# Two more sets of seven block products, third blocks asked for earlier, and more partner half tiles

## The chip, the cores and the metric

The kernel runs on one core of one Trainium2 chip. The metric is the device time of one execution in microseconds (us), as a median of runs. Five engines work on a core, each in its own program order, and wait for one another through semaphores: TensorE (PE in the profile, with its weight loads as PEld), VectorE (DVE), ScalarE (ACT), GpSimd (POOL) and SyncE (SP). DMA transfers are issued here by SP, by POOL and a few by ACT; a DMA stands in its issuer's queue, and a wait of the DMA holds what stands behind it in that queue.

## What is computed

One decoder layer on 256 tokens of width 2048, in float32 (cut to what matters):

```
h    = rmsnorm(x, pre_norm_g)                       # 256 x 2048
proj = h @ w_in                                     # a_q a_k a_v a_g a_lr b_q b_k b_v b_g m_a m_b
gk   = log_sigmoid(a_lr @ gla_gk_w2 + gla_gk_b) / 16
o_a  = rmsnorm(gated_linear_attention(a_q, a_k, a_v, gk), gla_norm_g) * silu(a_g)
o_b  = rmsnorm(differential_attention(b_q, b_k, b_v, lam), diff_norm_g) * (1 - lam_init) * silu(b_g)
merged = sigmoid(m_a) * (o_a @ w_branch_a) + sigmoid(m_b) * (o_b @ w_branch_b)
x + rmsnorm(merged @ w_out, post_norm_g)
```

The projection has 18,448 columns, the three matrices behind it 2048 each. The differential attention has 16 heads; the kernel treats them in four groups g of four, and each group in two pairs.

## The kernel before, in words

**Split operands.** A float32 product is made of three TensorE products: weights and activations are each split into a rounded part (hi) and the rest (lo), and hi*hi, hi*lo and lo*hi are added in PSUM. The x side is split once (tiles `xs`). Each weight is split as it comes: half a tile of 128x2048 at a time, ACT writes `hi` (L236) and DVE subtracts to get `lo` (L237). Both have three buffers, and the splits of a half tile are written four half tiles ahead of its matmuls (`AHEAD`, `take`).

**Plain half tiles.** `token_major` (matmuls on L413) makes 512 columns for the 256 tokens: eight half tiles of 12 matmuls. `channel_major` (L433 and L435) makes 128 columns with tokens along the free axis: two half tiles of 16 matmuls each.

**Block products.** A *set* makes two 256x512 results from one 2048x1024 weight with the 2x2 scheme that needs seven block products in place of eight (`PRODUCTS`, order 1, 3, 5, 6, 2, 7, 4). Each product has four half tiles of six matmuls (L666). The weight is cut into four blocks: `a` and `b` are tiles of 128x2048 by SP (`link`, four buffers), `c` is loaded by SP in four pieces of 128x1024 (L181) when product 2 reaches the split, and another block is added into `a` after product 1 and into `b` after product 6 by a DMA that accumulates, issued by POOL (L193). DVE makes a+b for product 6 (L184) and adds c into a behind each split of product 2 (L191). Product 4 accumulates into the same PSUM bank that DVE has just read for product 7.

**The joint phase.** Three sets run (`SETS = 3`): two for the branch-b merge gate, one for the values and gates (`dv0`, `bg0`) of head group 0. `phase_steps` puts *partner* half tiles between their 84 steps, spread evenly: `v4` (8 half tiles, token major) and `k` and `q` of the linear attention (32, channel major), 40 in all. Results of the sets go to DRAM by `spill` (a DMA on POOL) and come back by `fetch` (POOL too).

**After the phase.** Four `ag` tiles, m00, m01, head groups 0 and 1, the branch-a product `y0`, head groups 2 and 3, m02, m03, then `y1` and `o`. Groups 1 to 3 make `dv` and `bg` as plain tiles. Between half tiles `pump` lets small tasks go one step on: the forget gate, the scores and outputs of the linear attention, the attention pairs (`diff_pair`: scores L877/878, maxima on DVE L882, exponentials on ACT L888, weights L895, transposes L899, values L907 to L909, norm with a power on POOL L327, L920, transposes L925). In front of half tile 6 of the first `y1` tile, `settle` runs all tasks that are left to their end. A scheduling layer then settles the order on each engine.

Of the kernel before, what the change touches and what calls it, by code (L numbers as in the profile page):

```python
# [14 lines left out]
P = 128  # L15
# [13 lines left out]
SETS = 3  # L29
# [57 lines left out]
def hybrid_kernel(ctx: ExitStack, tc, xt, xn, preg, postg, w, w2, gkb, glag, lamv, diffg, ident_d, causal_d, lmask_d, out):  # L87
# [60 lines left out]
    def heads_order(g):  # L148
        values = (f"dv{g}", f"bg{g}") if g + 2 >= SETS else ()
        return halves_of(*values, *(f"{name}{g}{c}" for pair in range(2) for name in ("dq", "dk") for c in (2 * pair, 2 * pair + 1)))  # L150
# [20 lines left out]
    def emit_set(s, prod, t, h):  # L171
# [7 lines left out]
        if prod == 2:  # L179
            raws[s, t, h] = u([P, 1024], "c")  # L180
            sp.dma_start(raws[s, t, h], weights(f"set{s}", 4 + t)[0][:, c])  # L181
# [417 lines left out]
    ts = {}  # L599

    def others():
# [7 lines left out]
        for hf in range(2):  # L609
            for name in ("k", "q"):  # L610
                ts[name, hf] = u([P, 2, 4, P], name)
                for c in range(4):
                    o = ps("bg")
                    for h in range(2):
                        half_channel(o, h, *take(f"{name}{hf}{c}"))
                        if h:
                            o1, o2 = (t.rearrange("p (b t) -> p b t", b=2) for t in (o[:, :S], o[:, S:]))
                            t = ts[name, hf][:, :, c, :]
                            act.activation(t, o2, AF.Copy)
                            dve.tensor_tensor(out=t, in0=o1, in1=t, op=ALU.add)  # L620
# [10 lines left out]
    def block_products(s):  # L631
        x = ps("mm")
        bank = {1: x, 6: x, 7: x, 4: x}
        left, right = u([P, 2, 512], "gl"), u([P, 2, 512], "gr")
        kept = {}

        def right_done(b):
            dst = right[:, b, :]
# [7 lines left out]
        def left_done(b, src):  # L646
            if s < 2:
                act.activation(left[:, b, :], src, AF.Tanh, scale=half_rstd[:, b : b + 1])
            else:
                act.activation(left[:, b, :], src, AF.Copy, scale=rstd[:, b : b + 1])  # L650

        for prod in PRODUCTS:
# [3 lines left out]
            for t in range(2):  # L656
                for h in range(2):
# [10 lines left out]
                    if t and h:  # L668
# [6 lines left out]
                        if prod == 6:  # L675
                            dve.tensor_tensor(out=right[:, 0, :], in0=x, in1=kept[3], op=ALU.add)
                            right_done(0)
                        if prod == 2:
                            dve.tensor_tensor(out=left[:, 0, :], in0=out, in1=kept[1], op=ALU.add)
                            left_done(0, left[:, 0, :])  # L680
                        if prod == 7:
                            dve.tensor_tensor(out=right[:, 1, :], in0=x, in1=kept[5], op=ALU.add)
                            right_done(1)
                            gspill[2 * s + 1] = spill(right, "gr")
                        if prod == 4:
                            left_done(1, x)
                            gspill[2 * s] = spill(left, "gl")
# [20 lines left out]
    def gla_scores(hf, q, k):  # L708
# [80 lines left out]
    for hf in range(2):  # L789
        tasks.append(gla_scores(hf, ts["q", hf], ts["k", hf]))  # L790
# [58 lines left out]
    def diff_split(g, pair, tq, tk, q2, kh, kl):  # L849
# [11 lines left out]
    def diff_pair(g, pair, q2, kh, kl, vv, uu):  # L861
        oh, ol = obh[g], obl[g]
        cm = causal.rearrange("p a t -> p (a t)")
        cuts = ((0, P), (P, 3 * P))
        while f"split{g}{pair}" not in done:
            yield
        for h in (2 * pair, 2 * pair + 1):
# [60 lines left out]
        split_out(bank, hi, lo, diffg_s)  # L928
        yield

    def diff_heads(g):
        if g + 2 < SETS:
            vv, uu = (fetch(gspill[2 * g + 4 + i], name, u) for i, name in enumerate(("dv", "ub")))
        else:
# [7 lines left out]
            for b in range(2):  # L942
                gate(banks[b], b, uu[:, b, :])
        obh.append(u2([P, 4, S], "obh", F32R))
        obl.append(u2([P, 4, S], "obl", F32R))
        for pair in range(2):
            ts = []
            for name in ("dq", "dk"):
                t = t2([P, 2, S], name)
                for c in range(2):  # L950
                    o, o2 = channel_major(f"{name}{g}{2 * pair + c}")
                    act.activation(t[:, c, :], o2, AF.Copy)
# [214 lines left out]
```

## Time and profile before

| | |
|---|---|
| median of 3 runs | 1133.51 us (1131.94 to 1133.74) |
| the profiled execution | 1133.58 us, span 1131.8 us |
| busy | PE 1117.8, DVE 784.2, ACT 653.6, POOL 77.5 us |
| matmuls | 5618 |
| DMA | 234.68 MB, mean 207 GB/s |
| joint phase in the trace | about 82 to 309 us |

The span is the time between the first and the last recorded instruction; 1.8 us of the execution lie outside. Busy TensorE time counts a matmul from its start to a modelled end, so consecutive matmuls overlap in it: the step from one matmul of 512 columns to the next is shorter than the mean duration shown for one. The granted clock (PEclk) is 1.00 at full speed. A line `A <- B` in a list of waits reads: A stood idle until B was done. In a timeline the note in brackets is the idle time before the instruction and what ended it.

### The profile page before, as it was taken

To read this page: it belongs to the slowest core of one execution; us is meant where nothing else is said; L and a number is where in the kernel's file an instruction comes from. 1 tells how busy PE (TensorE), PEld (TensorE's weight loads), DVE (VectorE), ACT (ScalarE), POOL (GpSimd) and SP (SyncE) were. 2 spreads that over 40 slices of the span, in tenths; PEclk is the share of its full clock that TensorE was granted. 3 is DMA by queue.
4 is the path that set the end of the run, shared out by engine and by line. 5 is a ranking of instruction groups with operands and counts; after the bars stand their busy time and mean duration, and the time that the engine had idled before them with its cause. 6 is when DMAs were issued, how large, how long until landed. Compare 5 with 4: busy or idle time off the path is not lost.

```text
span 1131.8 us, 14913 instructions
## 1 busy us (share of the span) xinstructions
PE 1117.8 (99%) x5618; PEld 957.4 (85%) x5618; DVE 784.2 (69%) x1112; ACT 653.6 (58%) x971; POOL 77.5 (7%) x109
## 2 busy tenths in 40 slices
PE   9999999999999999999999999999999999999996
PEld 8998888887888888888888888888888888888886
DVE  6878979778757996856676555557666765666463
ACT  7856766665666564656676455556655655444460
POOL 0101010001102100101010100000000100000000
PEclk9999999999999999999999999999999999999999
DMA  8799897687454556764455545555455565556752
GB/s 302 256 409 240 264 291 212 246 257 195 156 197 168 198 177 223 236 243 151 160 193 176 211 161 183 183 186 186 155 180 186 195 214 183 180 188 212 276 188 75
DMA packets 39512, 234.68 MB, mean 207 GB/s; under 512 B 4944, under 2 KB 6480, under 8 KB 16912
## 3 DMA queue, kind: packets, MB, share of 16 engines
q1 hardware_dynamic: 31968, 202.79, 50.6%
q0 software_dynamic: 6464, 29.63, 9.8%
q10 hardware_dynamic: 1008, 1.32, 0.4%
q8 instruction: 44, 0.72, 0.3%
q14 instruction: 28, 0.23, 0.1%
HBM read 223.23 MB, written 10.49 MB: 207 GB/s over the span
## 4 chain that ended last, share of the span: by engine, by line
PE 94%; DVE 2%; DMA 1%; issue 1%; ACT 1%; SPq 0%; DVEq 0%; POOLq 0%; POOL 0%; ACTq 0%
PE mm L413 51%; PE mm L433 10%; PE mm L666 9%; PE mm L435 5%; PE bg L433 4%; PE bg L435 2%; PE bg L396 2%; PE mm L381 2%; PE mm L396 2%; PE bg L413 2%; PE bg L766 1%; DMA c<-in_w_dram 1%; DVE lo L237 1%; PE bg L381 1%; PE bg L877 1%
## 5 line engine op out<-in xcount | busy, mean ns | idle before, releaser
L237 DVE TENSOR_TENSOR lo<-raw,hi 128x1024 fp32r<-128x1024 f32 (+3 forms) x339 | 409.4, 1209 | 250.6 <-ACT hi L236 245.1
L236 ACT ACTIVATE hi<-raw 128x1024 fp32r<-128x1024 f32 (+3 forms) x339 | 350.3, 1035 | 346.4 <-PE mm L413 217.5
L413 PE MATMUL mm<-hi,xs 128*128 128x512 f32 (+1 forms) x1024 | 251.4, 387 | 0.0
L413 PEld LDWEIGHTS mm<-hi,xs 128*128 128x128 f32 x1024 | 189.5, 188 | 33.1
L413 PE MATMUL mm<-lo,xs 128*128 128x512 f32 (+1 forms) x512 | 134.6, 385 | 0.0
L433 PE MATMUL mm<-xs,hi 128*128 128x512 f32 x512 | 133.1, 395 | 0.0
L413 PEld LDWEIGHTS mm<-lo,xs 128*128 128x128 f32 x512 | 96.1, 188 | 17.9
L433 PEld LDWEIGHTS mm<-xs,hi 128*128 128x128 f32 x512 | 92.1, 189 | 15.8
L435 PEld LDWEIGHTS mm<-xs,lo 128*128 128x128 f32 x512 | 69.8, 190 | 5.1
L435 PE MATMUL mm<-xs,lo 128*128 128x256 f32 x512 | 71.4, 282 | 0.0
L433 PE MATMUL bg<-xs,hi 128*128 128x512 f32 x256 | 66.7, 391 | 0.2 <-ACT hi L236 0.2
L237 DVE TENSOR_TENSOR lo<-a,hi 128x1024 fp32r<-128x1024 f32 x48 | 58.5, 1222 | 8.8 <-ACT hi L236 8.2
L236 ACT ACTIVATE hi<-a 128x1024 fp32r<-128x1024 f32 x48 | 50.7, 1059 | 20.6 <-PE mm L666 12.3
L433 PEld LDWEIGHTS bg<-xs,hi 128*128 128x128 f32 x256 | 48.3, 189 | 10.0 <-ACT hi L236 0.6
L413 PE MATMUL mm<-hi,obh 128*128 128x512 f32 x128 | 50.7, 396 | 0.0
L413 PE MATMUL mm<-hi,oah 128*128 128x512 f32 x128 | 50.6, 395 | 0.0
L413 PE MATMUL mm<-hi,oal 128*128 128x512 f32 x128 | 49.9, 390 | 0.0
L413 PE MATMUL mm<-hi,obl 128*128 128x512 f32 x128 | 49.9, 390 | 0.0
L888 ACT ACTIVATE prob<-prob,mx,score_scale 128x128 f32<-128x128 f32 x64 | 34.3, 537 | 21.9 <-DVE mx L883 21.8
L666 PE MATMUL mm<-hi,xs 128*128 128x512 f32 x144 | 40.2, 401 | 2.0 <-ACT hi L236 1.8
L413 PE MATMUL mm<-hi,mh 128*128 128x512 f32 x96 | 37.4, 390 | 0.0
L413 PE MATMUL mm<-hi,ml 128*128 128x512 f32 x96 | 37.4, 389 | 0.0
(285 smaller groups left out, 1669.8 us busy)
## 6 DMA issues: line engine op xcount, KB each, us to landing
raw<-in_w_dram SPq DMA_DIRECT2D x152, 1024.0 KB, 4.9
raw<-in_w_dram SPq DMA_DIRECT2D x14, 832.0 KB, 6.6
a<-in_w_dram SPq DMA_DIRECT2D x6, 1024.0 KB, 7.2
b<-in_w_dram SPq DMA_DIRECT2D x6, 1024.0 KB, 7.9
c<-in_w_dram SPq DMA_DIRECT2D x12, 512.0 KB, 9.1
a<-in_w_dram POOLq DMA_DIRECT2D x6, 1024.0 KB, 12.3
b<-in_w_dram POOLq DMA_DIRECT2D x6, 1024.0 KB, 10.8
raw<-in_w_dram SPq DMA_DIRECT2D x4, 800.0 KB, 10.3
```

The lines of the kernel that those rows point to most:

```text
L236: act.activation(hi_t[:, a:b], r[:, a:b], AF.Copy)
L237: dve.tensor_tensor(out=lo_t[:, a:b], in0=r[:, a:b], in1=f32(hi_t[:, a:b]), op=ALU.subtract)
L381: i = pe.matmul(out, lhs, rhs, start=first and n == 0, stop=last and n == len(pairs) - 1)
L396: i = pe.matmul(banks[g][b][:, :n], a[part][:, P * b : P * b + P], w[:, n * g : n * g + n], start=first, stop=last)
L413: i = pe.matmul(banks[b][:, :n], a[part][:, P * b : P * b + P], w[:, n * j : n * j + n], start=first, stop=last)
L433: i = pe.matmul(o, hi[:, c], x_pair(kt), start=kt == 0, stop=kt == KT - 1)
L435: i = pe.matmul(o[:, :S], lo[:, c], x_ops(kt)[0], start=False, stop=False)
L666: i = pe.matmul(out, a[part], w[:, 512 * j : 512 * j + 512], start=first, stop=last, skip_group_check=out is x)
L766: pe.matmul(o, xk[:, P * c : P * c + P], xq.rearrange("p (b c t) -> p b c t", b=2, c=4)[:, :, c, :], start=i == 0, stop=i == 1)
L877: pe.matmul(banks[m][:, lo:up], q2[:, m, i2, t], kh[:, m, i2, :n], start=True, stop=False)
L888: act.activation(prob[m][:, lo:up], prob[m][:, lo:up], AF.Exp, scale=score_scale[:, b : b + 1], bias=mx[:, i : i + 1], accum_out=z[:, i : ...
```

## The change

- Five sets in place of three: `dv` and `bg` of groups 1 and 2 become sets 3 and 4 (counted from 0) and are no plain tiles any more. All sets' results for groups 0 to 2 are fetched from DRAM when the first pair of the group asks for them.
- A `c` piece is asked for `LEAD = 6` set steps before its split, so from product 5 on.
- The partner half tiles grow from 40 to 64: the `dq` and `dk` of head group 0 (16) and `m00` (8) are made in the phase.
- `k` and `q`, the `dq` and `dk` of groups 0 to 2, three merge gates and three `y0` results go to DRAM and back.
- Until the forget gate is done, tasks advance after every half tile, not every second one; m02 moves in front of `y0`, and `y0` and m02, m03 advance two tasks at a time.

```diff
-SETS = 3
+SETS = 5
+LEAD = 6
+EARLY = (0,)
+STORED = (0, 1, 2)
...
 def phase_steps():
     keys = ["v4"] + [f"{name}{hf}{c}" for hf in range(2) for name in ("k", "q") for c in range(4)]
-    other = [(key, r, h) for key in keys for r in range(1 if key[0] in "kq" else 4) for h in range(2)]
+    keys += [f"{name}{g}{c}" for g in EARLY for pair in range(2) for name in ("dq", "dk") for c in (2 * pair, 2 * pair + 1)]
+    keys += ["m00"]
+    other = [(key, r, h) for key in keys for r in range(4 if key in ("v4", "m00") else 1) for h in range(2)]
...
-    seq += halves_of(*(f"ag{g}" for g in range(4)), "m00", "m01") + heads_order(0) + heads_order(1)
-    seq += halves_of(*(f"y0{g}" for g in range(4))) + heads_order(2) + heads_order(3) + halves_of("m02", "m03")
+    seq += halves_of(*(f"ag{g}" for g in range(4)), "m01") + heads_order(0) + heads_order(1) + halves_of("m02")
+    seq += halves_of(*(f"y0{g}" for g in range(4))) + heads_order(2) + heads_order(3) + halves_of("m03")
...
     def emit_set(s, prod, t, h):
-        if prod == 2:
-            raws[s, t, h] = u([P, 1024], "c")
-            sp.dma_start(raws[s, t, h], weights(f"set{s}", 4 + t)[0][:, c])
+        n = 4 * PRODUCTS.index(prod) + 2 * t + h + LEAD - 4 * PRODUCTS.index(2)
+        if 0 <= n < 4:
+            i, j = n // 2, n % 2
+            raws[s, i, j] = u([P, 1024], "c")
+            sp.dma_start(raws[s, i, j], weights(f"set{s}", 4 + i)[0][:, 1024 * j : 1024 * j + 1024])
...
     def token_major(key, n, ops, step=1, settle=None):
-            if q % 2:
+            if q % 2 or "gate" not in done:
                 pump(step)
...
+    def merge_gate(banks):
+        t = u([P, 2, 512], "mgate")
+        for b in range(2):
+            act.activation(t[:, b, :], banks[b], AF.Tanh, scale=half_rstd[:, b : b + 1])
+        m0.append(spill(t, "mgate"))
...
     def others():
-                ts[name, hf] = u([P, 2, 4, P], name)
+                part = u([P, 2, 4, P], name)
...
+                            if c == 3:
+                                ts[name, hf] = spill(part, name)
+        for g in EARLY:
+            for pair in range(2):
+                for name in ("dq", "dk"):
+                    t = t2([P, 2, S], name)
+                    for c in range(2):
+                        o = ps("bg")
+                        for h in range(2):
+                            half_channel(o, h, *take(f"{name}{g}{2 * pair + c}"))
+                            if h:
+                                head_part(t[:, c, :], o[:, :S], o[:, S:], name == "dk")
+                                if c:
+                                    heads[g, pair, name] = spill(t, name)
+                            yield
+        banks = [ps("bg"), ps("bg")]
+        for q in range(KT // 2):
+            half_tile(banks, 512, q, x_ops, *take("m00"))
+            if q == KT // 2 - 1:
+                merge_gate(banks)
+            yield
...
-    def gla_scores(hf, q, k):
+    def gla_scores(hf):
+        q, k = (fetch(ts[name, hf], name, u) for name in ("q", "k"))
...
-    def diff_pair(g, pair, q2, kh, kl, vv, uu):
+    def diff_pair(g, pair, values):
+        while g and not {f"pair{g - 1}{p}" for p in range(2)} <= done:
+            yield
+        if not values:
+            values.extend(fetch(gspill[2 * g + 4 + i], name, u) for i, name in enumerate(("dv", "ub")))
+        if g in STORED:
+            tq, tk = (fetch(heads[g, pair, name], name, lambda shape, name, dtype: t2(shape, name)) for name in ("dq", "dk"))
+            yield
+            yield from diff_split(g, pair, tq, tk)
...
-        banks = token_major(f"y0{g}", 512, a_ops)
+        part = fetch(m0[g], "part", u) if g < 3 else u([P, 2, 512], "part")
+        banks = token_major(f"y0{g}", 512, a_ops, 2)
...
+        if g < 3:
+            half_done.append(spill(part, "part"))
```

Three places show what stands where now. The first is SP's queue at the `c` pieces of set 2. Before (the last four `c` rows of the program; `raw` is a plain weight tile):

```order
L168 DMA b_2121<-in_w_dram 128x2048
L181 DMA c_2434<-in_w_dram 128x1024
L181 DMA c_2457<-in_w_dram 128x1024
L208 DMA raw_2370<-in_w_dram 128x2048
L208 DMA raw_2470<-in_w_dram 128x2048
L208 DMA raw_2566<-in_w_dram 128x2048
L208 DMA raw_2653<-in_w_dram 128x2048
L181 DMA c_2486<-in_w_dram 128x1024
L181 DMA c_2512<-in_w_dram 128x1024
L208 DMA raw_2714<-in_w_dram 128x2048
```

Now, for the same set:

```order
L216 DMA raw_2307<-in_w_dram 128x2048
L189 DMA c_2272<-in_w_dram 128x1024
L189 DMA c_2295<-in_w_dram 128x1024
L189 DMA c_2319<-in_w_dram 128x1024
L189 DMA c_2345<-in_w_dram 128x1024
L216 DMA raw_2418<-in_w_dram 128x2048
L216 DMA raw_2516<-in_w_dram 128x2048
```

The third and fourth piece stood behind four `raw` transfers and now stand ahead of the next ones; set 3 and set 4 have their own four rows further down (two and three `raw` rows lie between the first and the last of them, beside loads of `a` and `b`).

The second place is POOL's queue where the forget gate's weights (`w_raw`) are loaded. Before, in the middle of the last set, behind its accumulating transfers:

```order
L193 DMA b_2073<-in_w_dram 128x2048
L193 DMA b_2121<-in_w_dram 128x2048
L474 MEMSET w_raw_2837 128x1024
L476 DMA w_raw_2837<-in_w_dram 16x1024 x4
L121 DMA gr_2669<-gr_2138 128x1024
L121 DMA gl_2759<-gl_2137 128x1024
```

Now, behind the last set's results and m00's gate:

```order
L126 DMA gr_3878<-gr_3732 128x1024
L126 DMA gl_3957<-gl_3797 128x1024
L482 MEMSET w_raw_4018 128x1024
L131 DMA q_4025<-q_2053 128x1024
L126 DMA mgate_3978<-mgate_3975 128x1024
L484 DMA w_raw_4018<-in_w_dram 16x1024 x4
L131 DMA k_4027<-k_1652 128x1024
```

The load moved from within the phase to its end. On PE the first matmul that needs it (L499, before L491) stands 64 matmuls and two transposes behind m00's last one.

The third place is DVE at the last head's way from its weights (L895, now L951) to its output (L920, now L976). Before, in the rows that end with it:

```order
L895 SCALAR_TENSOR_TENSOR prob_754_8184<-prob_755_8185,c_8241,prob_754_8184 128x256
L237 TENSOR_TENSOR lo_8210<-raw_8207,hi_8209 128x1024
L1006 SCALAR_TENSOR_TENSOR part_5949<-mgate_8246,part_5949 128x512
L1006 SCALAR_TENSOR_TENSOR part_5949<-mgate_8247,part_5949 128x512
L237 TENSOR_TENSOR lo_8226<-raw_8207,hi_8225 128x1024
L237 TENSOR_TENSOR lo_8265<-raw_8262,hi_8264 128x1024
L237 TENSOR_TENSOR lo_8281<-raw_8262,hi_8280 128x1024
L237 TENSOR_TENSOR lo_8305<-raw_8302,hi_8304 128x1024
L916 SCALAR_TENSOR_TENSOR de_8344<-dssq_8340,de_8344 128x2
L918 TENSOR_TENSOR de_8344<-de_8344,half_rstd 128x2
L920 SCALAR_TENSOR_TENSOR ogb_8134<-bg_8336,de_8344,ub_7345 128x128 x2
```

Now:

```order
L951 SCALAR_TENSOR_TENSOR prob_819_8512<-prob_820_8513,c_8535,prob_819_8512 128x256
L245 TENSOR_TENSOR lo_8585<-raw_8582,hi_8584 128x1024
L972 SCALAR_TENSOR_TENSOR de_8554<-dssq_8550,de_8554 128x2
L974 TENSOR_TENSOR de_8554<-de_8554,half_rstd 128x2
L976 SCALAR_TENSOR_TENSOR ogb_8462<-bg_8546,de_8554,ub_7665 128x128 x2
L245 TENSOR_TENSOR lo_8601<-raw_8582,hi_8600 128x1024
```

Five weight splits stood in between before and one stands there now. On PE it is 25 matmuls of 512 columns between that head's scores and its first transpose, three between its transposes and its value product, and seven (with two transposes) between that product and the first transpose of the output; before, 24 or more stood in each of these places.

More of the change, by code (lines that the diff above doesn't have):

```diff
@@ L633, in block_products @@
         bank = {1: x, 6: x, 7: x, 4: x}
[L634 to L635 removed]
+        kept, halves = {}, {}
         def right_done(b):
[L638 removed]
+            dst = halves["r"][:, b, :]
             if s < 2:
@@ L998, in hybrid_kernel @@
                 act.activation(t, banks[b], AF.Copy)
+        if g < 3:
+            half_done.append(spill(part, "part"))
     diff_heads(2)
     diff_heads(3)
-    for g in range(2, 4):
-        t = merge_gate(g, lambda b: t2([P, 512], "mgate"))
-        for b in range(2):
-            dve.scalar_tensor_tensor(out=part[g][:, b, :], in0=t[b], scalar=1.0, in1=part[g][:, b, :], op0=ALU.add, op1=ALU.mult)
+    banks = token_major("m03", 512, x_ops, 2)
+    for b in range(2):
+        t = t2([P, 512], "mgate")
+        act.activation(t, banks[b], AF.Tanh, scale=half_rstd[:, b : b + 1])
+        dve.scalar_tensor_tensor(out=part[:, b, :], in0=t, scalar=1.0, in1=part[:, b, :], op0=ALU.add, op1=ALU.mult)
+    parts_a = []
     gb = []
@@ L1012, in settle @@
             pump()
-        gb.extend(fetch(d, "gateb", u) for d in gspill[:4])
+        for g in range(4):
+            gb.append(fetch(gspill[g], "gateb", u))
+            parts_a.append(fetch(half_done[g], "part", u) if g < 3 else part)
     mh = [u([P, 4, S], "mh", F32R) for _ in range(4)]
```

87 lines of the change are left out of this document (44 added, 43 removed).

## The prediction

> **What bounds the kernel now.** I read the page first: its busy times and its chain that ended last.
>
> ```profile
> span 1131.8 us, 14913 instructions
> PE 1117.8 (99%) x5618; PEld 957.4 (85%) x5618; DVE 784.2 (69%) x1112; ACT 653.6 (58%) x971; POOL 77.5 (7%) x109
> PE 94%; DVE 2%; DMA 1%; issue 1%; ACT 1%; SPq 0%; DVEq 0%; POOLq 0%; POOL 0%; ACTq 0%
> ```
>
> TensorE carries 94% of the chain. So a change is worth the TensorE time it removes, less the new waits of TensorE. Next came the list of what TensorE waited for (total us, times, longest).
>
> ```profile
> PE mm L666 <- ACT hi L236: 1.8, 2, 1.5
> ...
> PE bg L827 <- DVE ua L820: 0.2, 1, 0.2
> ```
>
> Behind its start TensorE waits nearly nowhere, but for one place on L666, a block product. Its timeline there:
>
> ```profile
> 276.41 1.11 PE L435 MATMUL bg<-xs,lo 128*128 128x256 f32 x8
> 279.06 1.20 PE L666 MATMUL mm<-hi,xs 128*128 128x512 f32 x4 [1.54 <-ACT hi L236]
> 280.32 1.12 PE L666 MATMUL mm<-lo,xs 128*128 128x512 f32 x2
> 281.64 2.08 PE L666 MATMUL mm<-hi,xs 128*128 128x512 f32 x4 [0.21 <-ACT hi L236]
> ...
> 286.94 0.40 PE L666 MATMUL mm<-hi,r3h 128*128 128x512 f32 x1
> ```
>
> The same stretch by microseconds (time; busy PE, PEld, DVE, ACT, POOL; granted clock; DMA share; GB/s) and the queue that was late:
>
> ```profile
> 280.00:281.00 1.00, 0.94 (x4) 0.40 (x2) 0.81 (x2) 0.47 (x1) 0.00 (x0) 0.73 0.00 0
> 281.00:282.00 1.00, 0.79 (x3) 0.36 (x2) 1.00 (x2) 1.00 (x2) 0.00 (x0) 0.50 0.00 0
> 283.00:284.00 1.00, 1.00 (x4) 0.73 (x3) 1.00 (x2) 0.73 (x2) 0.00 (x0) 0.56 0.00 0
> 284.00:285.00 1.00, 1.00 (x6) 0.83 (x5) 1.00 (x1) 0.82 (x1) 0.00 (x0) 1.00 0.25 33
> ...
> 244.51 24.63 SPq L208 DMA_DIRECT2D raw<-in_w_dram  x3
> 269.19 0.96 SPq L181 DMA_DIRECT2D c<-in_w_dram  x2
> ...
> 269.78 10.65 DMA c<-in_w_dram
> ```
>
> SP stood 24.6 us in loads of plain weights; two `c` pieces of set 2 left only at 269.2, and the last took 10.65 us. ACT had nothing to split, TensorE waited 1.54 and 0.21 us, and the granted clock fell to half for three microseconds more.
>
> **What the sets remove.** Per group, 2 x 8 plain half tiles of 12 matmuls (192) become 28 set half tiles of 6 (168). The steps come from the chain, whose pieces leave the overlap out:
>
> ```profile
> 287.10 2.74 PE mm L666 x12
> 289.84 1.81 PE bg L433 x8
> 291.66 0.95 PE bg L435 x8
> ...
> 332.16 54.43 PE mm L413 x240
> ```
>
> A plain matmul takes 54.43/240 = 0.2268 us, one of a set 2.74/12 = 0.2283. Two groups save 2 x (192 x 0.2268 - 168 x 0.2283) = 2 x (43.55 - 38.35) = **10.4 us**. All other TensorE work is moved, not changed: a channel half tile costs 1.81 + 0.95 = 2.76 us wherever it stands.
>
> **The c pieces.** Had `c` been there, TensorE would have gone on at 276.41 + 0.95 = 277.36, done two set half tiles and one channel half tile (1.37 + 1.37 + 2.76), and been at 282.86. The next product began at 286.94: the place costs 4.1 us, 1.75 of it waiting and 2.3 slow clock. Now a piece leaves six set steps earlier. A step is 1.37 us and 64/140 = 0.457 partner half tiles of 2.76, so 2.63 us; six are 15.8 us, more than the 10.65 us of the slow transfer, and on SP the four pieces stand together, not behind four loads. I take **-4.1 us**, and nothing for late pieces in the new sets.
>
> [...]
>
> **What is late next there: DVE.** With `c` in time the four operations that DVE waited with would have run earlier, but not at once. The windows of five microseconds ahead of the wait, and DVE's timeline at it:
>
> ```profile
> 255.00:260.00 5.00, 5.00 (x27) 4.24 (x27) 5.00 (x6) 3.23 (x4) 0.87 (x1) 1.00 0.34 54
> 260.00:265.00 5.00, 5.00 (x27) 4.24 (x26) 5.00 (x7) 3.34 (x4) 0.86 (x1) 1.00 1.07 283
> ...
> 274.89 0.42 DVE L620 TENSOR_TENSOR q<-bg,q 128x256 f32<-128x256 f32 x1
> 277.87 1.23 DVE L191 TENSOR_TENSOR a<-a,c 128x1024 f32<-128x1024 f32 x1 [2.56 <-DMA c<-in_w_dram]
> 279.04 1.22 DVE L237 TENSOR_TENSOR lo<-c,hi 128x1024 fp32r<-128x1024 f32 x1
> ```
>
> DVE is busy without a gap through products 6 and 2, whose half tiles each need a split and an addition. It was through at 275.31; two additions and two splits at 1.17 us apart end at 279.99. TensorE wants the last of these at 277.36 + 1.37 + 4 x 0.228 = 279.64. So about 0.3 us of wait remains in a set that also has the gate's DVE operation of sets 2 to 4: three times 0.3, **+0.9 us**. From below zero (sets 0 and 1, with the same loads, show no wait on DVE); from above 4.1 us in each of the three, should a wait grow to the one measured, 12.3 us. I take the computed value. The slightly thinner mix (0.457 partners per step against 40/84 = 0.476) adds little: over eight steps DVE's 2.34 + 1.55 x share exceeds TensorE's 1.37 + 2.76 x share by 3.4 us in place of 3.2.
>
> **The forget gate's start.** Its weights are now asked for behind m00's gate on POOL. The rows of their load and preparation, and of a gate's two tanh:
>
> ```profile
> L476 POOL DMA_DIRECT2D w_raw<-in_w_dram x4: 487/496/529, 271.6 to 273.1; - x4
> L480 ACT ACTIVATE w_s<-w_raw x1: 1046/1046/1046, 294.5 to 294.5; 64x1024 fp32r<-64x1024 f32 x1
> L481 ACT ACTIVATE w2h<-w_raw x1: 1061/1061/1061, 297.3 to 297.3; 64x1024 fp32r<-64x1024 f32 x1
> L482 DVE TENSOR_TENSOR w_s<-w_raw,w2h x1: 1223/1223/1223, 298.4 to 298.4; 64x1024 fp32r<-64x1024 f32 x1
> DMA to landing us min/median/max: 5.9/6.5/7.3
> ...
> 942.48 1.24 ACT L975 ACTIVATE mgate<-mm,half_rstd 128x512 f32<-128x512 f32 x2
> ...
> a<-in_w_dram POOLq DMA_DIRECT2D x6, 1024.0 KB, 12.3
> ```
>
> From m00's end: 1.24, some 0.9 for issuing the spill (POOL's 0.87 in the window above), three issues of 0.5 before the fourth, 7.3 to land, 1.05 + 1.06 + 1.22: 14.3 us. TensorE has 64 x 0.2268 = 14.5 us of other work. The cover is just enough; ACT and DVE wait there with the next splits queued behind. I take **+0.5 us**; below it nothing, above it a landing like the accumulating transfer's 12.3: 5 us late and 2.3 of slow clock, 7.
>
> **The linear attention's outputs.** Two heads now pass at once where one did; before, their transposes waited 0.2 us for DVE. I take **+0.3**, from nothing to 1.8 (a wait as at `c`).
>
> **The last head.** In the second `y1` half nothing is left between its steps but what the change shows on DVE and PE. Their durations, from the last head before:
>
> ```profile
> 936.29 0.28 PE L878 MATMUL bg<-kl,q 128*128 128x256 f32 x1
> ...
> 942.12 0.75 DVE L895 SCALAR_TENSOR_TENSOR prob<-prob,c,prob 128x128 f32<-128x128 f32 x2
> ...
> 947.32 0.49 PE L899 MATMUL bg<-ident,prob 128*128 128x128 f32 x3
> ...
> 947.85 0.49 ACT L901 ACTIVATE wt<-bg 128x384 f32<-128x384 f32 x1 [0.18 <-PE bg L899]
> ...
> 953.56 0.39 PE L909 MATMUL bg<-dv,wt 128*128 128x128 f32 x2
> ...
> 955.95 0.61 DVE L920 SCALAR_TENSOR_TENSOR ogb<-bg,de,ub 128x128 f32<-128x128 f32 x2
> ```
>
> Scores to half of the weights: 936.41 to 942.5, 6.1 us, against 25 x 0.2268 = 5.7: 0.4 of wait. Transposes to copy: 1.0, against 0.9: 0.1. Values to the first half of the output: 953.7 to 956.25, 2.55 us, against seven matmuls and two transposes, 1.8: 0.7; its second half 0.3 later. **+1.5 us**; at least 0.5 (the last step alone, with ACT free), at most 3.8 if the waits together halve the clock once.
>
> **At no cost:** 24 more splits and 16 more additions (40 x 1.22 = 49 us on DVE, 25 on ACT) and 56 more POOL transfers (26 MB) lie beside TensorE, which hides them as it hides 784 us of DVE now; uncovered, 1.22 us each. The spilled tiles are fetched 20 us and more ahead of use.
>
> **Sum,** against the profiled execution's 1133.6 (span 1131.8 and 1.8 outside; the median is 1133.5): 1133.6 - 10.4 - 4.1 + 0.9 + 0.5 + 0.3 + 1.5 = 1122.3, so **1122 us**.
>
> **Rivals.** *No new waits:* the scheduler's order covers them all, as it did nearly everywhere before: 1119. *Cover gone at the tails:* the gate's start at its 7 or the last head at 3.8, or both in part: 1125 to 1131, say 1128. For it: the gate's margin is 0.2 us by my rows. *The request doesn't come earlier:* a buffer or SP's order still holds the pieces, and sets 2 to 4 all pay 4.1: 1133.6 - 10.4 + 8.2 + 2.3 = 1133.7, no change. Against it: SP's new order. *DVE sets the pace in the sets:* its lag through products 6 and 2 outgrows the four half tiles of lead, in each set, from the point where the wait left over is 1.5 us in place of 0.3; each then costs 4.1. Five sets: 1122.3 - 0.9 + 20.5 = 1142, **slower**; three sets: 1134. For it: 5.00 of 5.00; against it: sets 0 and 1 have the same loads and no such wait, and the lag grows by 0.2 us.
>
> **Chances.** The forecast (1119.5 to 1125) 0.58; no new waits 0.13; tails 0.15; late pieces 0.04; DVE in three sets 0.05, in five 0.05. A measurement here tells about 0.2% (2.3 us) from no change. Faster: the first three and a little, 0.88; within it 0.06 (late pieces and half of the three-set case); slower 0.06. The range 1117 to 1129 leaves out the last three cases and the ends of two others.
>
> **What will show it.** 5570 matmuls; the phase ends near 446 us (140 x 1.37 + 48 x 2.76 + m00's 22 + v4's 17 behind 82); no wait on `c`, or a wait of ACT for DMA `c` in sets 2 to 4 (wrong); waits of L706 on DVE, of L499 on DVE's `w_s`, of L955 and L981 on DVE, each of the size given. The granted clock below 1.00 anywhere between 100 and 1100 us would make a term too small; a saving other than 10.4 would show in the steps of L706.

## The result, and the profile after

| | before | changed |
|---|---|---|
| median, four runs each | 1133.62 us | 1123.04 us (1121.82 to 1124.39) |
| ratio, with its 95% interval | 1 | 0.9911 (0.9897 to 0.9925) |
| the profiled execution, and its span | 1133.58, 1131.8 us | 1123.60, 1121.8 us |

The forecast was 1122 us within 1117 to 1129. The profiled execution fell by 10.0 us; the sum had said 11.3. First the page's span and busy times of the changed kernel:

```profile
span 1121.8 us, 15070 instructions
PE 1105.6 (99%) x5570; PEld 945.4 (84%) x5570; DVE 831.8 (74%) x1160; ACT 677.1 (60%) x997; POOL 111.8 (10%) x165
```

Against the rows of before, TensorE is busy for 12.2 us less (1117.8 to 1105.6) and idle for 2.2 us more (1131.8 - 1117.8 = 14.0, now 1121.8 - 1105.6 = 16.2). So the gain is in work that is gone and in a clock that is not halved; the waits have become more, not fewer. Part of it is not the change's. The first matmul of the first set (before, then now):

```profile
82.08 1.09 PE L666 MATMUL mm<-hi,xs 128*128 128x512 f32 x4
80.84 1.09 PE L706 MATMUL mm<-hi,xs 128*128 128x512 f32 x4
```

What stands ahead of it is the same program. TensorE's first matmuls step at 0.35 us or more and the later ones at 0.19; the step changes at 10.8 us in the execution of before and between 6.4 and 7.7 us, in a wait, in the changed kernel's. Among the profiled executions of the runs below, two reach the first set at 82.2 us (four sets; m02 behind the heads) and the others at 80.5 to 81.0, so this belongs to the single execution and not to the change; it is worth 1.2 us here. From the first set on, the span fell by 8.8 us, not by 10.0.

The list of what TensorE waited for (total us, times, longest):

```profile
PE bg L321 <- DVE ones_b L318: 1.6, 1, 1.6
PE bg L981 <- DVE ogb L976: 1.5, 2, 0.9
PE bg L443 <- DVE lo L245: 0.8, 1, 0.8
PE mm L706 <- DVE gr L724: 0.8, 2, 0.5
PE mm L421 <- DVE lo L245: 0.7, 2, 0.5
PE bg L404 <- ACT hi L244: 0.7, 1, 0.7
PE bg L955 <- DVE prob L951: 0.3, 1, 0.3
```

The wait of a block product for ACT's `hi` (1.8 us before) is gone, and nothing waits for `c`. The new rows are small and stand in three regions. Their places, from TensorE's timeline; the last note of a row is the wait ahead of it:

```profile
140.94 1.19 PE L706 MATMUL mm<-hi,xs 128*128 128x512 f32 x4 [0.51 <-DVE gr L724]
257.01 1.21 PE L443 MATMUL bg<-xs,lo 128*128 128x256 f32 x8 [0.81 <-DVE lo L245]
...
463.92 1.19 PE L499 MATMUL bg<-lrt,w_s 128*128 128x256 f32 x8
...
711.55 0.59 PE L981 MATMUL bg<-ident,ogb 128*128 128x128 f32 x2 [0.91 <-DVE ogb L976]
...
952.79 0.33 PE L955 MATMUL bg<-ident,prob 128*128 128x128 f32 x1 [0.26 <-DVE prob L951]
957.54 0.33 PE L981 MATMUL bg<-ident,ogb 128*128 128x128 f32 x1 [0.57 <-DVE ogb L976]
```

Behind the start, the granted clock is 1.00 in every stretch of five microseconds up to the last one, where TensorE is done; before, 280 to 285 us had 0.66. The phase ended at 448.9 us.

### The profile page after: what moved, and what is told of

Read it like the earlier page. It is cut to its first block, busy times and chain, and to the rows that moved or that the text cites. A ratio compares the mean times of both kernels' runs of the same rounds, so it can differ in the third digit from the quotient of the medians.

```text
span 1121.8 us, 15070 instructions
## 1 busy us (share of the span) xinstructions
PE 1105.6 (99%) x5570; PEld 945.4 (84%) x5570; DVE 831.8 (74%) x1160; ACT 677.1 (60%) x997; POOL 111.8 (10%) x165
## 5 line engine op out<-in xcount | busy, mean ns | idle before, releaser
L245 DVE TENSOR_TENSOR lo<-raw,hi 128x1024 fp32r<-128x1024 f32 (+3 forms) x307 | 369.1, 1205 | 183.8 <-ACT hi L244 180.8
L244 ACT ACTIVATE hi<-raw 128x1024 fp32r<-128x1024 f32 (+3 forms) x307 | 315.8, 1032 | 282.0 <-PE mm L421 144.6
L421 PE MATMUL mm<-hi,xs 128*128 128x512 f32 (+1 forms) x704 | 171.4, 385 | 0.0
L421 PEld LDWEIGHTS mm<-hi,xs 128*128 128x128 f32 x704 | 130.2, 188 | 21.2
L245 DVE TENSOR_TENSOR lo<-a,hi 128x1024 fp32r<-128x1024 f32 x80 | 97.2, 1221 | 19.0 <-ACT hi L244 18.0
L244 ACT ACTIVATE hi<-a 128x1024 fp32r<-128x1024 f32 x80 | 84.7, 1059 | 39.4 <-PE mm L706 20.0
L441 PE MATMUL bg<-xs,hi 128*128 128x512 f32 x384 | 99.5, 390 | 0.2 <-ACT hi L244 0.2
L421 PE MATMUL mm<-lo,xs 128*128 128x512 f32 (+1 forms) x352 | 91.9, 383 | 0.7 <-DVE lo L245 0.7
L421 PEld LDWEIGHTS mm<-lo,xs 128*128 128x128 f32 x352 | 65.8, 188 | 12.9 <-DVE lo L245 1.6
L706 PE MATMUL mm<-hi,xs 128*128 128x512 f32 x240 | 65.1, 393 | 0.8 <-DVE gr L724 0.8
L443 PEld LDWEIGHTS bg<-xs,lo 128*128 128x128 f32 x384 | 52.3, 190 | 4.9 <-DVE lo L245 1.2
L443 PEld LDWEIGHTS mm<-xs,lo 128*128 128x128 f32 x384 | 52.4, 190 | 3.8
L245 DVE TENSOR_TENSOR lo<-b,hi 128x1024 fp32r<-128x1024 f32 x40 | 48.6, 1221 | 8.5 <-ACT hi L244 7.8
L443 PE MATMUL bg<-xs,lo 128*128 128x256 f32 x384 | 53.6, 282 | 0.8 <-DVE lo L245 0.8
L443 PE MATMUL mm<-xs,lo 128*128 128x256 f32 x384 | 53.5, 282 | 0.0
L706 PEld LDWEIGHTS mm<-hi,xs 128*128 128x128 f32 x240 | 44.4, 188 | 9.7 <-DVE gr L724 1.5
L421 PE MATMUL mm<-hi,oah 128*128 128x512 f32 x128 | 50.7, 396 | 0.0
L421 PE MATMUL mm<-hi,obh 128*128 128x512 f32 x128 | 50.7, 399 | 0.0
L421 PE MATMUL mm<-hi,obl 128*128 128x512 f32 x128 | 50.1, 392 | 0.0
```

Of the source, the lines that this page charges most:

```text
L244: act.activation(hi_t[:, a:b], r[:, a:b], AF.Copy)
L245: dve.tensor_tensor(out=lo_t[:, a:b], in0=r[:, a:b], in1=f32(hi_t[:, a:b]), op=ALU.subtract)
L421: i = pe.matmul(banks[b][:, :n], a[part][:, P * b : P * b + P], w[:, n * j : n * j + n], start=first, stop=last)
L441: i = pe.matmul(o, hi[:, c], x_pair(kt), start=kt == 0, stop=kt == KT - 1)
L443: i = pe.matmul(o[:, :S], lo[:, c], x_ops(kt)[0], start=False, stop=False)
L706: i = pe.matmul(out, a[part], w[:, 512 * j : 512 * j + 512], start=first, stop=last, skip_group_check=out is x)
```

## The experiments

The theory at the start was that of the prediction: 48 matmuls, the late `c` pieces with the half clock behind them, and DVE as what is late next. The rivals were that the clock's part of the second term has another cause, that the last two sets only break even, and that something other than DVE is the next deadline in a set. Each run below stands against runs of the kernel before on the same chip. The change itself was not run again beside them, so a microsecond or two between it and one of them is not told by the medians.

**The lead alone.** In the kernel before, with three sets:

```diff
-        if prod == 2:
-            raws[s, t, h] = u([P, 1024], "c")
-            sp.dma_start(raws[s, t, h], weights(f"set{s}", 4 + t)[0][:, c])
+        n = 4 * PRODUCTS.index(prod) + 2 * t + h + LEAD - 4 * PRODUCTS.index(2)
+        if 0 <= n < 4:
+            i, j = n // 2, n % 2
+            raws[s, i, j] = u([P, 1024], "c")
+            sp.dma_start(raws[s, i, j], weights(f"set{s}", 4 + i)[0][:, 1024 * j : 1024 * j + 1024])
```

> The kernel before with three sets and its own partners; only the c pieces are asked for six set steps earlier. Theory (the late c pieces of set 2 cost a wait of 1.75 us and 2.3 us of halved clock): both go, 0.3 us of wait on DVE is left there, so 3.8 us less than before, near 1129.8 us, granted clock 1.00 at 280 to 284 us. Rival 1 (the clock falls there for another reason than the wait): only 1.75 us less, near 1131.8, and the rows with 0.50 stay. Rival 2 (DVE is as late as c was, since its work runs without a gap there): no change, near 1133.5, and the wait stands on DVE's lo.

Measured: 1128.04 against 1132.37 us, ratio 0.9959 (0.9942 to 0.9975); the span fell from 1131.8 to 1127.5, 4.3 us, of which 1.3 us lie ahead of the first set (its first matmul starts at 80.77 us) and 3.0 behind. TensorE's timeline and the windows where the stall had been (time; busy PE, PEld, DVE, ACT, POOL; granted clock; DMA share; GB/s):

```profile
275.72 1.22 PE L438 MATMUL bg<-xs,lo 128*128 128x256 f32 x8 [0.20 <-DVE lo L240]
...
275.00:280.00 5.00, 4.80 (x26) 3.76 (x25) 5.00 (x7) 3.23 (x4) 0.00 (x0) 1.00 0.24 50
280.00:285.00 5.00, 5.00 (x26) 4.07 (x25) 5.00 (x6) 2.36 (x4) 0.00 (x0) 1.00 0.58 193
```

The wait and the half clock went together, so the wait had caused the half clock; what DVE still holds up is 0.20 us (L438 is the change's L443). The first theory stands, both rivals fall: 1.75 us alone would have been too little.

**The change without its lead.**

```diff
-LEAD = 6
+LEAD = 0
```

> The changed kernel with LEAD = 0: each c piece is asked for at its own split, as before. Theory: SP's order again holds the third or fourth piece of sets 2 to 4 behind plain weights, so ACT waits for DMA c and TensorE waits 1 to 1.8 us for ACT's hi in at least one set, with the clock halved behind it; one such set costs 4.1 us (1127), three cost 12.3 (1135). Rival (in the new mix the pieces come in time anyway, so that the lead is worth nothing): 1123 as the change, no wait on c.

Measured: 1131.20 us, ratio 0.9983 (0.9973 to 0.9993). Without the lead the change is worth 0.2%. One place pays, in set 1 and not in the three last: the timelines of DVE and TensorE, and the windows at it:

```profile
194.65 1.22 DVE L199 TENSOR_TENSOR a<-a,c 128x1024 f32<-128x1024 f32 x1 [6.91 <-DMA c<-in_w_dram]
...
197.06 2.08 PE L443 MATMUL bg<-xs,lo 128*128 128x256 f32 x8 [4.67 <-DVE lo L245]
...
195.00:196.00 1.00, 0.00 (x0) 0.00 (x0) 1.00 (x2) 0.79 (x1) 0.00 (x0) 0.93 0.98 401
196.00:197.00 1.00, 0.00 (x0) 0.00 (x0) 1.00 (x2) 0.30 (x1) 0.00 (x0) 0.50 0.05 16
```

DVE's addition of `c` stands in its queue ahead of the `lo` of the next partner, so TensorE waits at a partner, 4.67 us, for a transfer that the partner doesn't use. The clock is at half for 6.8 us (195.9 to 202.7), 5.6 of them behind the wait, so by these numbers this one place costs an estimated 4.67 + 2.8 = 7.5 us, nearly twice the 4.1 us expected for one place, and about the 7.6 us between the spans (1129.4 and 1121.8).

**One set fewer.** `SETS = 4` in the changed kernel.

> The changed kernel with four sets: dv and bg of group 2 are plain tiles again, all else as changed. Theory (each set is worth 24 matmuls): 5594 matmuls, 5.2 us more less 0.3 to 0.5 of one set's waits on DVE, so 1127.8 to 1128.3. Rival (the gain comes from the order around the sets, the fourth and fifth only break even since DVE pays in waits what the matmuls save): within 1 us of 1123.

Measured: 1132.52 us, ratio 0.9999 (0.9986 to 1.0011): 9.5 us above the change, which neither theory gives. The phase has no wait of TensorE any more; the loss lies elsewhere, in the heads of group 2 (ACT's timeline, then TensorE's, then its windows):

```profile
824.91 0.63 ACT L900 ACTIVATE kh<-dk 64x512 fp32r<-64x512 f32 x1 [2.71 <-DMA dk<-dk]
...
826.22 0.28 ACT L969 ACTIVATE junkd<-bg 128x128 bf16<-128x128 f32 x1
...
830.00 0.30 PE L933 MATMUL bg<-kh,q 128*128 128x128 f32 x1 [3.21 <-DVE ogb L976]
...
831.00:832.00 1.00, 1.00 (x4) 0.88 (x4) 1.00 (x1) 0.00 (x0) 0.00 (x0) 0.50 0.30 41
```

ACT stood for the second `dk` of a pair to come back from DRAM, and the square for the norm (L969) of another head stood behind it. That head's output came late, its bank was not free, and the next scores waited 3.21 us, with the clock at half from 830.2 to 833.6. Whether the round trip was to blame needed a run of its own.

**One set fewer, and group 2 kept on the chip.**

```diff
-SETS = 5
+SETS = 4
-STORED = (0, 1, 2)
+STORED = (0, 1)
```

> Four sets as in e3_four, and the dq and dk of head group 2 stay on the chip in place of a round trip through DRAM. Theory (in e3_four 5.2 us were the 24 matmuls, and the rest was this round trip: ACT waited for DMA dk, the square behind it in ACT's queue and so the last output of a head were late, TensorE waited 3.2 us and 1.9 us went to half clock): that wait goes, 1132.5 - 5.1 = 1127.4. Rival (the head's tail is late whatever the round trip): 1132.

Measured: 1127.72 us, ratio 0.9968 (0.9953 to 0.9984); the 3.2 us and the half clock are gone. The fifth set is then worth 4.7 us by the medians, and 6.5 by the two ratios, each against the kernel before on its own chip. By the profiled executions, which reach the first set 0.1 us apart, it is 1125.4 - 1121.8 = 3.6 us, and 5.4 with the 1.8 us of waits that five sets have in the phase and four have not; TensorE's busy time fell by 3.5 (1109.1 to 1105.6). The 5.2 us priced for 24 matmuls lie within these, and the runs don't tell it closer. (Edits that move the order around the sets can cost as much as a set brings: that was the error in reading the run before this one.)

**Fewer partners.**

```diff
-EARLY = (0,)
+EARLY = ()
```

> The changed kernel with 48 partner half tiles in place of 64: the dq and dk of head group 0 are made behind the phase. The matmuls stay 5570. Theory (DVE lags through products 6 and 2 and partners give it the time): at 0.34 partners a step the lag over eight steps is 8 x (2.34 - 1.37 - 1.21 x 0.34) = 4.5 us in place of 3.4, so 1.1 us more wait in each of five sets, 5.5 us, and 2.3 more wherever a wait halves the clock: 1128 to 1135. Rival (the buffers' lead covers it, the waits of 0.26 to 0.81 us in the changed kernel have other causes): 1122 to 1123.5, the tails having 16 half tiles more to hide in.

Measured: 1146.59 us, ratio 1.0122 (1.0103 to 1.0142), worse than any theory had it (the profiled execution, 1141.97, is the fastest of the four). In the list of ACT's waits one row has grown from 3.5 us in the changed kernel (first row) to 16.9 (second); below it the largest stall, on POOL, ACT and TensorE:

```profile
ACT hi L244 <- DMA a<-in_w_dram: 3.5, 2, 2.5
...
ACT hi L244 <- DMA a<-in_w_dram: 16.9, 5, 7.4
...
351.95 0.88 POOL L201 DMA_DIRECT2D a<-in_w_dram  x1 [2.44 <-DVE lo L245]
...
371.26 1.06 ACT L244 ACTIVATE hi<-a 128x1024 fp32r<-128x1024 f32 x1 [7.36 <-DMA a<-in_w_dram]
...
372.37 0.79 PE L706 MATMUL mm<-hi,r1h 128*128 128x512 f32 x1 [3.67 <-ACT hi L244]
```

It isn't DVE that is late first, but the accumulating transfer into `a`: issued behind product 1, wanted at product 5, and here 19.3 us under way. Between the two lie only the four steps of product 3 and their partners. DVE is late too, but by 0.7 us at most.

**Partners where DVE is behind.** The changed kernel with its 64 partners three times as dense from the middle of product 5 to the middle of product 2:

```diff
+    weight = [3 if 10 <= i % 28 < 18 else 1 for i in range(len(steps))]
     for i, step in enumerate(steps):
         mixed.append(step)
-        mixed += other[len(other) * i // len(steps) : len(other) * (i + 1) // len(steps)]
+        a, b = sum(weight[:i]), sum(weight[: i + 1])
+        mixed += other[len(other) * a // sum(weight) : len(other) * b // sum(weight)]
```

> The changed kernel with the same 64 partners, three times as dense in the eight steps from the middle of product 5 to the middle of product 2 (0.84 a step) and thinner in the others (0.28). Theory 1 (the waits of 0.81, 0.51 and 0.26 us in the changed kernel are DVE's lag through products 6 and 2): the lag of 8 x (0.97 - 1.21 x share) is gone, so are these waits: 1121 to 1122. Theory 2 (from the thin kernel: what is late first is the accumulating transfer into a, issued behind product 1 and wanted at product 5, 15 us and more to land): product 3 has 4 x (1.37 + 2.76 x 0.28) = 8.6 us in place of 10.5, so ACT waits for DMA a, 2 us and more in several sets, TensorE 1 to 2 us in each, with half clock behind it: 1128 to 1136.

Measured: 1131.93 us, ratio 0.9999 (0.9986 to 1.0011). Theory 2, by ACT's and TensorE's lists (L708 and L246 here are the change's L706 and L244):

```profile
ACT hi L246 <- DMA a<-in_w_dram: 20.1, 6, 5.3
...
PE mm L708 <- ACT hi L246: 4.0, 3, 2.6
PE bg L445 <- DVE lo L247: 1.5, 2, 0.8
```

And DVE's waits did not go either. With product 3 thinned, the transfer is late, and at one of the two places where TensorE waits for a `lo` (411 us) ACT had waited 3.60 us for the transfer just ahead, so that DVE started late; at the other (257 us) it had not.

**Partners for both.** As above, with weight 2 from product 3 to the middle of product 2 (`2 if 4 <= i % 28 < 18 else 1`).

> The changed kernel with the same 64 partners, twice as dense from product 3 to the middle of product 2 (0.61 a step) and 0.30 in the others, so that both the accumulating transfer into a and DVE get more time. Theory (either of the two, it needs no choice): no wait of TensorE for ACT or DVE in the phase, the 1.8 us of the changed kernel are gone: 1121.2. Rival (the waits stand at the set's ends, at products 7 and 4 where this mix is thinner: 0.51 and 0.26 us were for gr): they grow to 1 us a set, 1125.

Measured: 1124.22 us, ratio 0.9936 (0.9921 to 0.9951), no better than the change. ACT's waits for the transfer are 2.4 us in all and no `lo` is late in the phase, but the rival came in one place, at the end of a set (DVE, then TensorE):

```profile
217.23 0.68 DVE L726 TENSOR_TENSOR gr<-mm,p 128x512 f32<-128x512 f32 x1
...
218.06 1.84 PE L708 MATMUL mm<-hi,xs 128*128 128x512 f32 x4 [3.19 <-DVE gr L726]
```

Product 4 adds into the bank that DVE must first read for product 7's `gr`. Here no partner stands between the two products, and TensorE waits for what stands ahead of that addition in DVE's queue: the third deadline of a set, and the one behind the 0.51 and 0.26 us in the changed kernel. A partner there helps, but is not sure cover: in the order of the traces, whole half tiles of 16 matmuls stand between products 7 and 4 at those two waits, and only 4 matmuls in set 1, which has no wait. It is also a matter of how much DVE has to do first.

**Partners at fixed places.** Thirteen places for every set, of which one always lies between products 7 and 4 (after step 23):

```diff
     for i, step in enumerate(steps):
         mixed.append(step)
-        mixed += other[len(other) * i // len(steps) : len(other) * (i + 1) // len(steps)]
+        if i % 28 in (1, 3, 5, 7, 9, 11, 12, 14, 16, 18, 20, 23, 26) and not (i // 28 >= 4 and i % 28 == 20):
+            mixed.append(other.pop(0))
```

> The changed kernel with the same 64 partners at the same thirteen places of every set (twelve in the last): every second step, one more in product 6, and always one between products 7 and 4. Theory (three deadlines make the phase's waits: the accumulating transfer into a before product 5, DVE through products 6 and 2, and DVE's gr before product 4, which has cover only where a partner stands between 7 and 4): all three have cover, the waits of 0.81, 0.51, 0.26 and 0.20 us go, span 1120.0 and time 1121.2. Rival (the waits come from where ACT and DVE stand in their queues and move elsewhere): 1122 to 1124 with as much waiting as in the changed kernel.

Measured: 1123.49 us, ratio 0.9923 (0.9893 to 0.9953). Between 80 and 450 us the list of TensorE's waits is empty, as the theory of the three deadlines had it. But two of the four runs stand at 1120.5 and 1121.3, with a mean granted clock of 0.998, and two at 1125.7 and 1126.8, with 0.995 and 0.994. The profiled execution is the longest one and shows why (the landing times of the forget gate's weights in the changed kernel, then here; TensorE at the gate, and windows):

```profile
DMA to landing us min/median/max: 7.0/7.1/7.6
...
DMA to landing us min/median/max: 12.3/12.6/12.9
...
464.71 0.55 PE L501 MATMUL bg<-lrt,w_s 128*128 128x256 f32 x1 [4.03 <-issue]
...
463.00:464.00 1.00, 0.00 (x0) 0.00 (x0) 0.62 (x1) 0.98 (x2) 0.00 (x0) 0.82 0.99 397
469.00:470.00 1.00, 1.00 (x4) 0.71 (x4) 0.16 (x1) 1.00 (x2) 0.94 (x2) 0.50 0.93 393
```

POOL had issued the loads at 448.0, 3.3 us earlier than in the changed kernel, just behind a spill of the last set; they took 12.6 us in place of 7.1, and TensorE waited 4.0 us at the gate. The DMA engines were full in both kernels (a share of 1.02 here and 0.99 there from 450 to 455 us), so that alone doesn't explain the longer time; what does is open.

**The gate's weights asked for earlier.** As the last, with `w2_raw` allocated and loaded in front of the sixth half tile of m00:

```diff
         for q in range(KT // 2):
+            if q == 5:
+                w2_early.append(u([P, 1024], "w2_raw"))
+                pool.memset(w2_early[0], 0.0)
+                for i in range(4):
+                    pool.dma_start(w2_early[0][32 * i : 32 * i + RANK, :], w2)
             half_tile(banks, 512, q, x_ops, *take("m00"))
```

> e9_placed5 with the forget gate's weights asked for before the sixth half tile of m00, in the phase, and so ahead of its last results on POOL, the merge gate's spill and the fetches of q and k. Theory (in e9_placed5 the transfer landed after 12.6 us in place of 7.1, TensorE waited 4.0 us and the clock was half for 6 us, in some executions only): no execution pays this, the phase stays without waits, so every run stands where the better ones of e9_placed5 stood, 1120.5 to 1121.5, with a median near 1121, 2 us less than the changed kernel. Rival (the spread of e9_placed5 has another cause): the runs again lie at 1120.5 and at 1126, median 1123.

Measured: 1123.92 us over six runs, ratio 0.9925 (0.9907 to 0.9944). Five of the six lie between 1123.59 and 1124.02, the sixth at 1126.19. That most of the spread has gone fits the theory that it was the load, but the runs at 1120.5 have gone too, and the 2 us did not come. The phase has no waits, but at the gate, which now comes at 454.4 us in place of 463.9, TensorE waits 0.5 us, and behind it more (TensorE, then ACT):

```profile
487.56 1.19 PE L423 MATMUL mm<-lo,xs 128*128 128x512 f32 x4 [1.89 <-DVE lo L247]
...
489.82 0.85 ACT L792 ACTIVATE ath<-att 128x768 fp32r<-128x768 f32 x1 [5.39 <-POOL att L772]
```

The scores of the linear attention wait on POOL, and ACT's next splits stand behind `ath`. The waits from 480 to 495 us are 3.2 us, where the changed kernel has 0.7 among the same scores (at 494 and 500 us).

**m02 behind the heads again.**

```diff
-    ... heads_order(0) + heads_order(1) + halves_of("m02")
-    ... heads_order(2) + heads_order(3) + halves_of("m03")
+    ... heads_order(0) + heads_order(1)
+    ... heads_order(2) + heads_order(3) + halves_of("m02", "m03")
```

with m02's gate applied there, as m03's.

> The changed kernel with m02 behind head group 3 again, beside m03, as before. Theory (the last heads are drained in the second y1 half tile because four pumps fewer stand ahead of it: 0.6 us for the output and 0.3 us for the weights): with m02's eight half tiles there these 0.9 us go, and the wait of 0.9 us at the first y0 tiles stays or moves: 1122.1. Rival (the rate of two tasks at a time sets the tail): no change, 1123. Against both: the first heads then lose eight half tiles of cover ahead of y0, where a drain would cost 1 us and more: 1124 to 1126.

Measured: 1123.00 us, ratio 0.9922 (0.9905 to 0.9940), no difference from the change that the runs can tell. (Its profiled execution has the late start, 82.21 us at the first set, and is 1.5 us shorter than the changed kernel's from there on.) The three waits at the heads' ends (0.91, 0.57 and 0.26 us) are gone, and TensorE's list has others in their place:

```profile
PE bg L870 <- DVE oal L459: 1.0, 1, 1.0
PE bg L933 <- ACT kh L901: 0.5, 1, 0.5
```

**A sixth set.** `SETS = 6`, with the 64 partners at ten or eleven fixed places of a set (after steps 1, 4, 6, 8, 10, 12, 14, 16, 19, 23, 26); and the same with m02 behind the heads.

> As e9_placed5 with a sixth set (dv and bg of head group 3), so the 64 partners stand at ten or eleven places of a set, chosen by the same rule: two in product 3, two in each of 5, 6 and 2, one between 7 and 4. 5546 matmuls. Theory (places matter more than the share, 0.38 a step, at which the even mix was late): 5.4 us less by matmuls, up to 2 us of waits on DVE since the lag over eight steps is 8 x 0.97 - 4 x 2.42 x 0.5 = 2.9 us, and 1 to 2 us in the tails, which lose 16 plain half tiles of cover: 1118 to 1120. Rival (DVE or the transfer into a sets the pace at this share, as in the thin kernel): 1128 or more.

> As e10_placed6 with m02 behind head group 3, as in e8_m02_behind. Theory (the tails lack cover in front of the second y1 half tile, and m02's eight half tiles give four pumps there): 1 us less than e10_placed6 if that one waits 1 us or more at the last heads. Rival (what is gained there is lost at the first heads, as in e8_m02_behind): the same within 0.5 us.

Measured: 1130.24 us, ratio 0.9986 (0.9968 to 1.0004), and 1131.32 us, 0.9994 (0.9979 to 1.0009). The phase itself is not what loses: in the first of the two its waits of TensorE are 2.0 us. The list of the whole has, among others:

```profile
PE bg L983 <- DVE ogb L978: 2.9, 3, 1.1
PE bg L957 <- DVE prob L953: 2.2, 3, 0.9
PE mm L423 <- DVE lo L247: 1.7, 2, 1.3
```

The heads' tails wait 5.1 us where the changed kernel has 1.8: a set takes 16 plain half tiles of cover from the tasks behind the phase as well. All waits listed sum to 6.8 us more than in the changed kernel (13.4 and 6.6), which is more than the 5.4 us of matmuls; the spans differ by 4.8 us the wrong way (1126.6), which leaves 3.4 us. Of these, 3.2 are TensorE's busy time: it fell by 2.2 us (1105.6 to 1103.4) and not by 5.4, with the clock at 1.00 through the phase and behind it, as in the changed kernel. Why its matmuls take longer there stays open. m02 behind the heads did not help.

## Why the prediction was right, point by point

**The matmuls, -10.4.** 5570 as said. TensorE's busy time fell by 12.2 us. Of these 1.6 lie ahead of the first set (it starts 1.2 us sooner, though TensorE has waited 0.3 us longer) and 1.7 are the half clock (3.41 us at half speed), so 8.9 us are left for the matmuls. The term was 1.5 us too large; its steps came from one place and one stretch of the trace.

**The c pieces, -4.1.** In the run with the lead alone 4.3 us, but 3.0 from the first set on. The mechanism is the one predicted: the wait and the half clock went. The size was too large, as the slow clock had been put at 2.3 us and 3.41 us at half speed lose 1.7. The half clock belongs to the term: a gain of 1.75 us is outside that run's interval (0.9975 of 1132.4 is 2.8 us less).

**DVE late next, +0.9.** The waits in the phase rose from about 0.5 us (0.3 for `gr`, 0.2 elsewhere) to 1.8, so +1.3. The size was near, the mechanism only partly right. DVE's lag through products 6 and 2 accounts for 0.81 us in one set, at a partner just ahead of product 6 and not at product 2's last split. The 0.51 and 0.26 us are the addition for `gr` in front of product 4, which the prediction did not have. And its step "what is late next is DVE" left out the accumulating transfer into `a`: at 0.34 partners a step, and with product 3 thinned, that one was late first. The rival of DVE setting the pace, with a slower end at 1142, had the right price and sign for a mix that is too thin (1147) under the wrong name.

**The gate's start, +0.5.** Nothing in the changed kernel. Its `w_s` was done by DVE at 462.6 + 1.2 = 463.8 and TensorE came at 463.9: a margin of 0.1 us, where 0.2 had been worked out. The upper bound of 7 us, from a landing of 12.3 in place of 7.3, is what the run with fixed places then met: 12.6 us, 4.0 of wait and the clock at half from 463.6 to 470.5. It was one move in the order away.

**The linear attention's outputs, +0.3.** No wait there. The 0.7 us lie some 120 us earlier, among its scores (L421 for DVE's `lo`, at 494 and 500 us; the outputs' transposes begin at 620). The 0.2 us of before have gone, so +0.5. The step named the wrong place.

**The last head, +1.5.** 0.8: 0.26 for the weights (0.4 said), nothing for the transposes (0.1), 0.57 for the output (0.7, and 0.3 for its second half, which cost nothing). Not in the sum at all: 0.91 us at a head that ends in the first `y0` tile, the same step in another place, and 0.3 us more at the start.

**At no cost.** The stored tiles did not all land ahead of use: ACT waited 1.3 us for `dk` and 1.1 us for `dq` in the changed kernel. TensorE didn't feel it there, but it did in the run with four sets, 3.21 us with the half clock behind.

**The sum.** Waits: -1.75 + 1.3 + 0.0 + 0.5 + 0.8 + 0.9 + 0.3 = 2.1 us more, near the 2.2 by which TensorE's idle time rose. With 12.2 us less of busy time that is the 10.0 us measured, 1.3 us less than forecast. Luck has a part in this: 1.2 us of the 10.0 are the start's, and the change itself is 2.5 us short of its 11.3, 1.5 in the matmuls and the rest in the `c` term and the waits. The new waits had been put at 3.2 us and came to 3.5 without the start's, but only the last head's stand where they were expected. The end of the phase was put at 446 us, from 82 on, and came at 448.9, from 80.8 on; 1.8 of it are waits. No rival came; the nearest, the tails' cover, needed a further edit to come.

## What to carry to other kernels

When TensorE is the bound, price a change twice: what its matmuls save, which came out within a microsecond a set for the two sets here (8.9 us against 10.4), and which queue's next deadline moves closer, which decides the sign; here every set has three (a transfer that accumulates into a block still to be used, an engine's lag through its double-work steps, a bank that must be read before the next product adds into it), and what covers each is the work that stands at that place, not the mean share of it. Then look at what the moved work had covered where it stood: a sixth set brought 3.3 us more of waits at the heads' tails, and more than half of its saving did not show in TensorE's busy time; no order tried for a microsecond of waits gained it in its median. A margin of 0.1 us on a transfer is no margin, as the same load took 7.1 us in one order and 12.6 in another. And compare single executions from a common point on: here 1.2 us of the difference lay ahead of anything that the change touches.

## What the runs showed of the hardware

In the thin kernel's execution the clock was at half twice; the windows of 0.2 us at the edges of the two (the sixth number is the granted clock):

```profile
372.20:372.40 0.20, 0.03 (x1) 0.03 (x1) 0.05 (x1) 0.20 (x2) 0.00 (x0) 0.79 0.00 0
375.60:375.80 0.20, 0.20 (x2) 0.20 (x1) 0.20 (x2) 0.00 (x0) 0.20 (x1) 0.68 0.00 0
839.80:840.00 0.20, 0.00 (x0) 0.00 (x0) 0.20 (x2) 0.20 (x2) 0.00 (x0) 0.86 0.00 0
843.20:843.40 0.20, 0.20 (x2) 0.16 (x1) 0.20 (x2) 0.00 (x0) 0.00 (x0) 0.61 0.83 328
```

Taking the clock as 1.00 or 0.50 within a window, it fell at 372.32 and 839.94 and rose at 375.73 and 843.36: 3.41 us each time. Windows of 1 us give 3.42 us by the same sum before (280.46 to 283.88), with four sets (830.20 to 833.62), with the partners where DVE is behind (101.76 to 105.18) and with the partners for both (218.30 to 221.72). TensorE's waits at these six places were 3.67 and 2.03 us in the thin kernel, then 1.54, 3.21, 2.61 and 3.19 us. The length of a wait doesn't settle whether the clock falls:

```profile
103.62 0.50 PE L706 MATMUL mm<-hi,r1h 128*128 128x512 f32 x1 [2.56 <-ACT hi L244]
```

This wait of 2.56 us in the thin kernel's execution left the clock at 1.00 (100 to 108 us), and so did the 1.89 us in the run with the gate's weights asked for earlier (485 to 495 us). What decides stays open. In these executions a wait of 1.5 to 3.7 us cost itself, or itself and, by an estimate from the 3.41 us at half speed, up to 1.7 us more of lost work; the waits of 4.7 us (without the lead) and 4.0 us (at the gate) had the half clock twice as long, 6.8 us.
